# Second block's attention: query remainders on VectorE, weight remainders on GpSimd, third query set transposed later

## The chip, the cores and the metric

The kernel runs on one core of a Trainium2 chip. The metric is the device time of one execution, in microseconds (us). One core has TensorE (matrix products; "PE" in the rows, its weight loads "PEld"), VectorE ("DVE"), ScalarE ("ACT"), GpSimd ("POOL"), and SyncE ("SP"), which here starts DMA transfers. Each engine executes its own instructions in the order in which they stand in the program, and waits for the others by semaphores.

## The reference

The input is 512 tokens by 1024 features, all in f32. It goes through a first block (two layers of gated recurrent and convolutional mixing with a feed-forward part) and a second block. The change is in the attention of the second block:

```python
h = rmsnorm(x, attn_norm_w)
a_q, a_k, a_v, i_q, i_k, i_w, b_q, b_k, b_v, g_a, g_b = split(h @ w_in)
# a: 8 query heads of 64, i: 8 index heads of 64, b: 8 query heads of 64;
# keys and values have 4 heads; i_k is one head with a layer norm
a_q, a_k, i_q, i_k, b_q, b_k = rope(...)
o_a = dsa_branch(a_q, a_k, a_v, i_q, i_k, i_w, 128)  # each query attends to 128 keys, by index scores
o_b = swa_branch(b_q, b_k, b_v, sinks)               # sliding window with a sink per head
mix = sigmoid(g_a) * (o_a @ w_branch_a) + sigmoid(g_b) * (o_b @ w_branch_b)
x = x + mix @ w_out
```

A feed-forward part and a last norm follow.

## The kernel before

**Products in three parts.** Every f32 product is made of three matmuls of a reduced f32 type: high by high, high by low and low by high parts (lines 202, 203, 204). So each operand is split in two: a copy in the reduced type, and the remainder that the copy lost. Weights come in chunks of 128 x 1024 by DMA, four chunks ahead of their use. `prep` (line 173) splits a chunk: ScalarE copies it (line 178), and the remainder is made either by VectorE in one operation (`self.V`) or by GpSimd in pieces of 256 columns (line 182). Which of the two is written in the string `pool` of the stage's entry in `TUNE`: it lists the indices of the chunks that go to GpSimd, one string for each weight matrix. The entry of the second block's attention is the fifth, line 29. Its nine strings stand for the index queries (4 chunks), the keys (3), the values (2), the queries of branch b (4), those of branch a (4), the gates of branch b (four matrices of 2 chunks), the gates of branch a, and the two output matrices. Before, the first six are empty.

**Queries.** `q_proj` makes one set of queries: 4 token tiles of 128 x 512, accumulated in 4 banks of PSUM over 4 chunks of weights (24 matmuls a chunk). `q_hold` then evacuates each tile: `rotate` (line 1127) multiplies it by cosines and, in two halves, by sines (VectorE, tiles named t), adds the two (line 1136, on GpSimd where the flag `pool` is set), ScalarE copies the sum as the high part (line 1147), and line 1148 subtracts for the remainder, on GpSimd. `q_turn` (line 1152) transposes the held tiles (line 1160, 8 transposes into a bank of tag "py", of which there are two, in the order of use shared with the gates' matmuls), and evacuates each bank by ScalarE (line 1166) or by VectorE's CAST. There are three such sets: index queries, branch b ("s" tiles), branch a ("E" tiles).

**Order of the stage.** `block2` emits: index queries, keys, values, index scores, then the queries of branch b and of branch a, then a loop over four head pairs of branch b. Each pass takes two pending turns from the list `turns`, emits a gate (24 matmuls, p<-hT,w), the scores of the next pair (lines 1244 and 1245, two matmuls each, whose row sums VectorE makes with small operations on two columns, c, behind them), a second gate, and the values of the present pair: transposes of the probabilities (line 1373), VectorE's split of the transposed tile (E<-p,E), and the matmuls of lines 1325 to 1327. Eight gates make 192 matmuls.

**Selection in the background.** `select` (line 1267) finds the 128 largest index scores of each query: 16 rounds of MAX (line 1275) and MATCH_REPLACE (line 1276) on three score rows of 256, 384 and 512 columns, ended by line 1278. It is spawned behind the index scores, and `pump` (line 133) puts its steps between other work: a step is emitted when VectorE's booked time and the step's cost stay within TensorE's booked time plus a slack of 8 us. Every operation called through `self.V` (class `Paced`, line 55) books VectorE time; one on GpSimd books none. A scheduler then orders each engine's queue.

Of the kernel before, what the change touches and what calls it, by code (L numbers as in the profile page):

```python
# [13 lines left out]
OP = mybir.AluOpType  # L14
# [11 lines left out]
        dict(slack=0.0, tap=400, prep=20, fetch=-50, ada=100, aq=0, ak=1, af=1, bp=1000, pt=1, adma=-300, gap=3.0, pool=('01', '01'), mv=(), early=1, pin=0, go=0, ho=1),  # L26
        dict(slack=12.0, tap=400, prep=50, fetch=-200, ada=800, aq=0, ak=0, af=0, bp=200, pt=0, adma=100, gap=3.0, pool=('01', '01', '01', '01', '0'), mv=(1, 0, 0), early=1, pin=1, go=0, ho=1),
        dict(slack=10.0, tap=1500, prep=-30, fetch=0, ada=0, aq=0, ak=1, af=1, bp=0, pt=0, adma=100, gap=3.0, pool=('01', '1'), mv=(), early=0, pin=0, go=0, ho=1),
        dict(slack=8.0, tap=200, prep=50, fetch=-200, ada=300, aq=1, ak=0, af=0, bp=200, pt=0, adma=100, gap=6.0, pool=('', '', '', '', '', '', '012', '01', ''), mv=(), early=0, pin=0, go=0, ho=1),
        dict(slack=8.0, tap=200, prep=50, fetch=-200, ada=300, aq=1, ak=0, af=0, bp=200, pt=0, adma=100, gap=6.0, pool=('', ''), mv=(), early=0, pin=0, go=0, ho=1)]  # L30

COLS = {}
# [18 lines left out]
def f32(ap):  # L51
    return ap.bitcast(F32)
# [20 lines left out]
class Kern:  # L73
# [1068 lines left out]

    def q_hold(self, i, p, hold, tag):

        a = self.rotate(p.rearrange("p (h d) -> p h d", h=8), i, 8, True)
        q = self.tile(tag, (128, 8, 128), F32R)
        self.nc.scalar.activation(q[:, :, 0:64], a, AF.Copy)
        self.nc.gpsimd.tensor_tensor(q[:, :, 64:128], a, f32(q[:, :, 0:64]), op=OP.subtract)
        hold[i] = q

    def q_turn(self, i, hold, qt, hps):
# [244 lines left out]
    def block2(self):  # L1396
        nc, V = self.nc, self.V
        qi = self.q_proj("s")
        kt = self.k_proj()
        vs = self.v_proj()  # L1400
        self.work_turns()
        self.index_scores(qi, kt[0])
        self.selected = False
        self.spawn(self.select())
        qb = self.q_proj("s")
        qa = self.q_proj("E")
        gb = [self.tile("ad", (128, 2, T)) for _ in range(3)] + [self.tile("E", (128, 2, T))]
        gb = [gb[j // 2][:, j % 2] for j in range(8)]
        ob = []
        P = self.scores_b(0, qb, kt)  # L1410
        for hp in range(4):
            for _ in range(2):
                if self.turns:
                    self.turns.pop(0)()
            self.gate(gb[2 * hp], "py")
            Q = self.scores_b(hp + 1, qb, kt) if hp < 3 else None
            self.gate(gb[2 * hp + 1], "py")
            ob.append(self.values_b(hp, P, vs))
            P = Q
        self.drain(lambda: self.selected)  # L1420
        oa, wb, ga = [], [], []
        heads = [1, 0, 3, 2, 5, 4, 7, 6]
        P = self.scores_a(heads[0], qa, kt)
        o = None
        for n, h in enumerate(heads):
            if n % 2 == 0:
                g = self.tile("E", (128, 2, T))
                ga += [g[:, 0], g[:, 1]]
                o = self.bank(tag="py")
            p = self.branch(n, wb, ob)  # L1430
            V.scalar_tensor_tensor(gb[n], gb[n], 1.0, p, op0=OP.add, op1=OP.mult)
            Q = self.scores_a(heads[n + 1], qa, kt) if n < 7 else None
            self.gate(ga[n], "pc")
            self.values_a(h, P, o, vs)
            if n % 2:
                oa.append(self.out_T(o))
            P = Q
        for n, o in (("oa", oa), ("ob", ob)):
            for k in range(4):
                if self.dump is not None and n + str(k) in self.dump:  # L1440
                    t = self.t2()
                    V.tensor_tensor(t, f32(o[k][:, 0]), f32(o[k][:, 1]), op=OP.add)
                    self.dbg(n + str(k), t)
        if self.stop == "att":
            return
        mix, wa = [], []
        for j in range(8):
            p = self.branch(j, wa, oa)
            t = self.t2()
            V.scalar_tensor_tensor(t, ga[j], 1.0, p, op0=OP.add, op1=OP.mult)  # L1450
            nc.gpsimd.tensor_tensor(t, t, gb[j], op=OP.add)
            s = self.slot((128, 2, T), F32R)
            self.split(s[:, 0], s[:, 1], t, 0.5)
            mix.append(s)
        self.y = [self.tile("E" if i < 4 else "s", (128, D)) for i in range(4)]
        for i in range(4):
            nc.sync.dma_start(self.y[i], self.xsrc[i])
        self.n += 1
        dst = self.dram.tile([T, D], F32, name=f"xd{self.n}")
        self.xsrc = [dst[i * 128:(i + 1) * 128, :] for i in range(4)]  # L1460
        self.tok_group(lambda k, i: (mix[k][:, 0, i * 128:(i + 1) * 128], mix[k][:, 1, i * 128:(i + 1) * 128]),
                       False, True, self.add_norm(self.cols2[:, 8:16]))
        if self.stop == "b2":
            return
        self.tune = TUNE[5]
        self.ffn(self.final_norm, onto_x=True)
# [225 lines left out]
```

## Time and profile before

| | |
|---|---|
| median of 3 runs | 2317.67 us (2316.12 to 2319.96) |
| profiled execution | 2312.6 us, span 2310.9 us |
| mean granted TensorE clock | 0.988 of full speed |
| TensorE busy | 2217.4 us, 96% of the span |
| VectorE busy | 1470.7 us, 64% |
| ScalarE busy | 972.4 us, 42% |
| GpSimd busy | 718.9 us, 31% |

The shares are over the whole span. The attention of the second block lies between about 1545 and 1800 us; the changed instructions there are a small part of the span, so the stretch itself has to be read: windows for the shares by stretch, and the engines' timelines for what an engine waited for.

### The profile page before, as it was taken

The numbers are of one execution on the slowest core, as the hardware profiler recorded it, in microseconds if no ns is written. First come the engines' busy times: TensorE is split into PE (matmuls) and PEld (weight loads), VectorE is DVE, ScalarE is ACT, GpSimd is POOL, SyncE is SP. The second block draws the span as 40 slices with busy tenths as digits, with TensorE's granted clock in tenths as the row PEclk, the third lists the DMA queues.
The fourth block names the chain that finished last, engine by engine and source line by source line (L and its number), as shares of the span: only waits on it lengthen the run. The fifth ranks groups of instructions, "written<-read, shape, count | busy, mean of one in ns | idle before, by whom it ended". The sixth has DMA issues, their size and how long they took to land.

```text
span 2310.9 us, 29330 instructions
## 1 busy us (share of the span) xinstructions
PE 2217.4 (96%) x10744; PEld 1813.1 (78%) x10744; DVE 1470.7 (64%) x2939; ACT 972.4 (42%) x1697; POOL 718.9 (31%) x934
## 2 busy tenths in 40 slices
PE   5998999899999999999999999999989999999998
PEld 3677887788888787788778888878778888888886
DVE  6699999637676769999663333357996445443434
ACT  3435554533223454555543322344456534332232
POOL 4645561515325454655351210212112340000000
PEclk8999999999999999999999999999999999999999
DMA  7424226346666432222323323232111234222222
GB/s 285 160 92 137 64 87 205 128 143 216 210 203 210 140 119 86 70 65 73 121 101 128 113 91 100 93 100 90 62 55 56 64 108 152 105 99 93 92 100 82
DMA packets 77759, 271.39 MB, mean 117 GB/s; under 512 B 9008, under 2 KB 9776, under 8 KB 77616
## 3 DMA queue, kind: packets, MB, share of 16 engines
q1 hardware_dynamic: 69840, 241.21, 31.3%
q0 software_dynamic: 7776, 28.32, 3.7%
q8 instruction: 84, 1.38, 0.2%
q14 instruction: 59, 0.48, 0.1%
HBM read 256.91 MB, written 12.58 MB: 117 GB/s over the span
## 4 chain that ended last, share of the span: by engine, by line
PE 77%; DVE 10%; ACT 4%; POOL 3%; issue 3%; DMA 2%; SPq 0%; ACTq 0%; POOLq 0%; DVEq 0%
PE p L202 24%; PE p L204 24%; PE p L203 24%; DVE p L872 2%; POOL w L182 2%; DVE c L69 1%; ACT w L178 1%; DVE E L69 1%; DVE w L69 1%; DMA ad<-in_ada_dram 1%; PE p L1244 1%; DVE cc L69 1%; DMA wr<-in_win_dram 1%; DVE s L69 1%; DVE e L1276 1%
## 5 line engine op out<-in xcount | busy, mean ns | idle before, releaser
L182 POOL TENSOR_TENSOR w<-wr,w 128x256 fp32r<-128x256 f32 x648 | 502.6, 808 | 699.2 <-ACT w L178 619.1
L178 ACT ACTIVATE w<-wr 128x1024 fp32r<-128x1024 f32 (+1 forms) x353 | 369.7, 1049 | 610.5 <-PE p L204 525.0
L202 PE MATMUL p<-hT,w 128*128 128x512 f32 (+1 forms) x1568 | 586.6, 376 | 16.2 <-ACT hT L214 9.8
L203 PE MATMUL p<-hT,w 128*128 128x512 f32 (+1 forms) x1568 | 584.6, 373 | 9.2 <-POOL hT L218 5.4
L204 PE MATMUL p<-hT,w 128*128 128x512 f32 (+1 forms) x1568 | 585.0, 374 | 0.8 <-POOL w L182 0.7
L202 PE MATMUL p<-w,s 128*128 128x512 f32 (+1 forms) x1152 | 449.2, 390 | 3.5 <-ACT s L214 3.5
L203 PE MATMUL p<-w,s 128*128 128x512 f32 (+1 forms) x1152 | 448.0, 389 | 0.6 <-DVE w L69 0.6
L204 PE MATMUL p<-w,s 128*128 128x512 f32 (+1 forms) x1152 | 446.8, 389 | 0.1
L69 DVE TENSOR_TENSOR w<-wr,w 128x1024 fp32r<-128x1024 f32 (+1 forms) x187 | 234.4, 1254 | 294.2 <-ACT w L178 293.8
L202 PEld LDWEIGHTS p<-hT,w 128*128 128x128 f32 x1568 | 297.2, 190 | 72.5 <-ACT hT L214 11.6
L203 PEld LDWEIGHTS p<-hT,w 128*128 128x128 f32 x1568 | 298.3, 190 | 64.4 <-POOL hT L218 6.5
L872 DVE SCALAR_TENSOR_TENSOR p<-ga,ad,p 128x495 f32<-128x495 f32 (+24 forms) x480 | 339.0, 729 | 7.3 <-ACT p L867 6.3
L204 PEld LDWEIGHTS p<-hT,w 128*128 128x128 f32 x1568 | 298.5, 190 | 56.0 <-POOL w L182 3.7
L202 PEld LDWEIGHTS p<-w,s 128*128 128x128 f32 x1152 | 216.6, 188 | 52.6 <-ACT s L214 4.5
L204 PEld LDWEIGHTS p<-w,s 128*128 128x128 f32 x1152 | 216.3, 188 | 49.6 <-DVE s L69 1.1
L203 PEld LDWEIGHTS p<-w,s 128*128 128x128 f32 x1152 | 216.4, 188 | 48.7 <-DVE w L69 1.1
L69 DVE TENSOR_TENSOR E<-p,E 128x512 f32<-128x512 f32 (+4 forms) x152 | 94.9, 638 | 147.9 <-PE p L204 119.7
L69 DVE SCALAR_TENSOR_TENSOR t<-p,t 128x512 f32<-128x512 f32 x96 | 65.9, 687 | 128.8 <-ACT t L1066 128.7
L319 DVE SCALAR_TENSOR_TENSOR ad<-ad,ad 128x1024 f32<-128x1024 f32 x80 | 110.3, 1384 | 42.6 <-DMA ad<-in_ada_dram 42.6
L1066 ACT ACTIVATE t<-p 128x512 f32<-128x512 f32 x96 | 56.6, 589 | 157.6 <-PE p L204 157.6
L69 DVE TENSOR_TENSOR s<-t,s 128x512 fp32r<-128x512 f32 (+1 forms) x100 | 99.2, 992 | 11.1 <-ACT s L1068 5.7
L612 POOL TENSOR_TENSOR E<-E,s 128x512 f32<-128x512 f32 x32 | 46.4, 1460 | 155.4 <-ACT j L610 155.4
(279 smaller groups left out, 2622.3 us busy)
## 6 DMA issues: line engine op xcount, KB each, us to landing
wr<-in_ff_dram SPq DMA_DIRECT2D x128, 512.0 KB, 3.6
wr<-in_win_dram SPq DMA_DIRECT2D x64, 512.0 KB, 3.6
ad<-in_ada_dram POOLq DMA_DIRECT2D x54, 512.0 KB, 4.8
wr<-in_wout_dram SPq DMA_DIRECT2D x40, 512.0 KB, 3.6
wr<-in_up_dram SPq DMA_DIRECT2D x32, 512.0 KB, 3.7
wr<-in_down_dram SPq DMA_DIRECT2D x32, 512.0 KB, 3.3
ad<-in_ada_dram SPq DMA_DIRECT2D x26, 512.0 KB, 4.4
xd<-E SPq DMA_DIRECT2D x20, 512.0 KB, 2.7
```

The costliest lines, as they stand in the source:

```text
L69: return f(out, *a, **kw)
L178: self.nc.scalar.activation(u[:, 0, :w], raw[:, :w], AF.Copy)
L182: self.nc.gpsimd.tensor_tensor(u[:, 1, o:e], raw[:, o:e], f32(u[:, 0, o:e]), op=OP.subtract)
L202: mm(out, lh, rh, start=first, stop=False)
L203: mm(out, lh, rl, start=False, stop=False)
L204: self.mm = mm(out, ll, rh, start=False, stop=last)
L319: return self.nc.vector.scalar_tensor_tensor(w, w, 1.0, self.cact, op0=OP.mult, op1=OP.mult, accum_out=m)
L612: nc.gpsimd.tensor_tensor(y[:, h], y[:, h], row[:, h], op=OP.mult)
L872: V.scalar_tensor_tensor(y[:, d:], a[:, :T - d], w[:, o - d:o - d + 1], y[:, d:], op0=OP.mult, op1=OP.add)
L1066: nc.scalar.activation(r, p, AF.Relu)
L1244: mm(out, q[h // 2][:, h % 2, tk], k[:, 0, keys], start=True, stop=False)
L1276: V.match_replace(self.sel[i], m, self.sel[i], TAKEN)
```

## The change

Three things change. The strings `pool` of the stage send the remainders of 22 more weight chunks to GpSimd: two chunks of the index queries, all three of the keys, one of the values, all eight of the queries of b and a, and all eight of the gates of branch b (four weight matrices of two chunks each). The sum of the rotation and the remainder of the 12 query tiles go from GpSimd to VectorE. The loop over head pairs takes no turns in its first pass, so the transposes of the third query set begin one pass later. The DMA transfers keep their order.

```diff
-        dict(slack=8.0, ..., pool=('', '', '', '', '', '', '012', '01', ''), ...),
+        dict(slack=8.0, ..., pool=('01', '012', '0', '0123', '0123', '01', '012', '01', ''), ...),
...
     def q_hold(self, i, p, hold, tag):
 
-        a = self.rotate(p.rearrange("p (h d) -> p h d", h=8), i, 8, True)
+        a = self.rotate(p.rearrange("p (h d) -> p h d", h=8), i, 8)
         q = self.tile(tag, (128, 8, 128), F32R)
         self.nc.scalar.activation(q[:, :, 0:64], a, AF.Copy)
-        self.nc.gpsimd.tensor_tensor(q[:, :, 64:128], a, f32(q[:, :, 0:64]), op=OP.subtract)
+        self.V.tensor_tensor(q[:, :, 64:128], a, f32(q[:, :, 0:64]), op=OP.subtract)
         hold[i] = q
...
         for hp in range(4):
-            for _ in range(2):
+            for _ in range(2 if hp else 0):
                 if self.turns:
                     self.turns.pop(0)()
             self.gate(gb[2 * hp], "py")
```

**VectorE at the third query set.** Of before, from the set's first rotation (t<-p,gw; s is a bank of the second set's transposes, w a weight remainder, ga and c the scores' row sums):

```order
L69 TENSOR_TENSOR t_14865<-p_14630,gw_11084 128x512
L69 TENSOR_TENSOR t_14866<-p_14630,gw_11084 128x8x32 x2
L69 ISA ga_14879,c_14880<-p_14878,ad_11086 128x128
L69 ISA c_14880 128x1
L69 CAST s_14967<-p_14976 128x2x256
L69 ISA ga_14879,c_14880<-p_14878,ad_11086 128x128
L69 ISA c_14880 128x1
L69 TENSOR_TENSOR w_14994<-wr_14729,w_14994 128x1024
L69 TENSOR_SCALAR c_14881<-c_14880 128x2
L69 CAST s_14969<-p_14988 128x2x256
```

Of the new kernel, from the same set's rotations (t<-t,t is the sum, E the remainder):

```order
L69 TENSOR_TENSOR t_14928<-p_14693,gw_11084 128x8x32
L69 TENSOR_TENSOR t_14936<-p_14694,gw_11084 128x512
L69 TENSOR_TENSOR E_14924<-t_14918,E_14924 128x8x64
L69 TENSOR_TENSOR t_14927<-t_14927,t_14928 128x512
L69 TENSOR_TENSOR t_14937<-p_14694,gw_11084 128x8x32 x2
L69 TENSOR_TENSOR E_14933<-t_14927,E_14933 128x8x64
L69 TENSOR_TENSOR t_14936<-t_14936,t_14937 128x512
L69 TENSOR_TENSOR t_14945<-p_14695,gw_11084 128x512
L69 TENSOR_TENSOR t_14946<-p_14695,gw_11084 128x8x32
L69 TENSOR_TENSOR E_14942<-t_14936,E_14942 128x8x64
L69 TENSOR_TENSOR t_14946<-p_14695,gw_11084 128x8x32
L69 ISA ga_14959,c_14960<-p_14958,ad_11086 128x128
```

The sums and the remainders stand between the rotations on VectorE now, and the weight remainder w has gone.

**VectorE at the values of head pair 0.** Of before, the rows up to the first split (E<-p,E), with two banks of the third set's transposes (s) and a weight remainder:

```order
L1276 MATCH_REPLACE e_14307<-cc_15809,e_14307 128x384
L69 TENSOR_SCALAR c_14947<-c_14946 128x2
L69 CAST s_14967<-p_15208 128x2x256
L69 TENSOR_TENSOR c_14949<-ad_11086,c_14947 128x2
L69 TENSOR_TENSOR w_15226<-wr_14997,w_15226 128x1024
L69 TENSOR_TENSOR c_14949<-c_14949,c_14948 128x2
L69 CAST s_14969<-p_15220 128x2x256
L69 RECIPROCAL c_14950<-c_14949 128x2
L69 ISA ga_15026,c_15027<-p_15025,ad_11086 128x128
L69 ISA c_15027 128x1
L69 TENSOR_TENSOR E_15150<-p_15145,E_15150 128x512
```

Of the new kernel, the rows up to the first split:

```order
L1278 TENSOR_SCALAR e_14333<-e_14333 128x256
L1276 MATCH_REPLACE e_14333<-cc_15922,e_14333 128x512
L69 TENSOR_TENSOR c_15129<-c_15129,c_15128 128x2
L1278 TENSOR_SCALAR e_14333<-e_14333 128x384
L69 RECIPROCAL c_15130<-c_15129 128x2
L69 ISA tc_15147,c_15148<-p_15146,ad_11086 128x256
L69 ISA c_15148 128x1
L1278 TENSOR_SCALAR e_14333<-e_14333 128x512
L69 ISA tc_15147,c_15148<-p_15146,ad_11086 128x256
L69 ISA c_15148 128x1
L69 TENSOR_SCALAR c_15149<-c_15148 128x2
L69 TENSOR_TENSOR E_15208<-p_15203,E_15208 128x512
```

and from the last split to the first bank of the third set's transposes:

```order
L69 TENSOR_TENSOR E_15248<-p_15245,E_15248 128x2x128
L69 TENSOR_SCALAR c_15347<-c_15346 128x2
L69 TENSOR_TENSOR c_15349<-ad_11086,c_15347 128x2
L69 TENSOR_TENSOR c_15349<-c_15349,c_15348 128x2
L69 RECIPROCAL c_15350<-c_15349 128x2
L69 ISA z_15367,c_15368<-p_15366,ad_11086 128x256
L69 ISA c_15368 128x1
L69 TENSOR_TENSOR s_15257<-p_15202,s_15257 128x512
L69 CAST s_15261<-p_15270 128x2x256
```

The end of selection (L1278) now stands ahead of the first split (before, 35 of its 99 rows stand behind), and the second bank's CAST, which stood ahead of the first split, stands behind the last.

**TensorE ahead of the 49th gate matmul.** Of before (p<-identr,E are transposes of the third query set; the gate matmul is p<-hT,w, and the 48th is a few rows up):

```order
L1160 MATMUL p_15220<-identr,E_14862 128x128
L1160 MATMUL p_15220<-identr,E_14871 128x128
L1160 MATMUL p_15220<-identr,E_14862 128x128
L1160 MATMUL p_15220<-identr,E_14871 128x128
L1325 MATMUL p_15144<-E_15150,s_14291 128x256
L202 MATMUL p_15231<-hT_13496,w_14782 128x512
```

Of the new kernel, where values and scores of pair 1 fill the place between the 48th and the 49th:

```order
L1326 MATMUL p_15202<-E_15248,s_14329 64x128
L1327 MATMUL p_15202<-E_15248,s_14329 64x128
L1373 MATMUL p_15473<-identr,z_15125 128x128
L1373 MATMUL p_15473<-identr,tc_15147 128x128
L1373 MATMUL p_15473<-identr,z_15125 128x128
L1373 MATMUL p_15473<-identr,tc_15147 128x128
L1244 MATMUL p_15366<-E_14064,s_14730 128x256
L1245 MATMUL p_15366<-E_14064,s_14730 128x256
```
```order
L1160 MATMUL p_15282<-identr,E_14933 128x128
L1160 MATMUL p_15282<-identr,E_14924 128x128
L1160 MATMUL p_15282<-identr,E_14933 128x128
L202 MATMUL p_15296<-hT_13502,w_14853 128x512
```

Before, 23 rows lie between the 48th and the 49th gate matmul; now 93 do.

## Rows read from the trace of the kernel before

**Rows 1.** Windows: length; busy us (count) PE, PEld, DVE, ACT, POOL; clock, DMA, GB/s.
```profile
1650.00:1675.00 25.00, 24.33 (x115) 19.52 (x114) 21.75 (x50) 7.53 (x10) 11.14 (x8) 1.00 0.19 68
1675.00:1700.00 25.00, 19.52 (x96) 16.10 (x94) 19.92 (x53) 8.75 (x19) 10.19 (x8) 0.80 0.18 65
1690.00:1695.00 5.00, 4.89 (x21) 4.19 (x20) 4.51 (x9) 2.51 (x8) 3.07 (x3) 0.50 0.25 90
1700.00:1725.00 25.00, 23.35 (x137) 19.25 (x135) 24.71 (x93) 18.22 (x53) 0.00 (x0) 1.00 0.12 43
```

**Rows 2.** TensorE's timeline: start us, length, line, operation, form [idle before, releaser].
```profile
1591.85 0.37 PE L1160 MATMUL p<-identr,s 128*128 128x128 f32 x2 [2.08 <-ACT s L1166]
...
1681.03 0.40 PE L204 MATMUL p<-w,hT 128*128 128x512 f32 x1
...
1685.65 0.34 PE L1160 MATMUL p<-identr,E 128*128 128x128 f32 x2 [1.71 <-ACT s L1166]
...
1689.16 1.00 PE L1160 MATMUL p<-identr,E 128*128 128x128 f32 x6 [2.87 <-POOL E L1148]
...
1692.78 0.79 PE L202 MATMUL p<-hT,w 128*128 128x512 f32 x1
...
1706.75 0.39 PE L204 MATMUL p<-hT,w 128*128 128x512 f32 x1
...
1711.57 0.50 PE L202 MATMUL p<-hT,w 128*128 128x512 f32 x1
...
1765.75 0.40 PE L204 MATMUL p<-hT,w 128*128 128x512 f32 x1
```

**Rows 3.** GpSimd's timeline: query sums and remainders, then weight pieces.
```profile
1682.14 1.27 POOL L1136 TENSOR_TENSOR t<-t,t 128x512 f32<-128x512 f32 x1 [15.30 <-DVE t L69]
...
1692.32 1.49 POOL L1148 TENSOR_TENSOR E<-t,E 128x512 fp32r<-128x512 f32 x1 [0.74 <-ACT E L1147]
...
1742.19 3.42 POOL L182 TENSOR_TENSOR w<-wr,w 128x256 fp32r<-128x256 f32 x4 [48.38 <-DVE c L69]
...
1752.79 2.81 POOL L182 TENSOR_TENSOR w<-wr,w 128x256 fp32r<-128x256 f32 x4 [7.17 <-ACT w L178]
```

**Rows 4.** VectorE's timeline, from the second query set to the end of selection.
```profile
1652.69 3.54 DVE L69 TENSOR_TENSOR t<-p,gw 128x512 f32<-128x512 f32 x8
...
1680.72 3.53 DVE L69 TENSOR_TENSOR t<-p,gw 128x512 f32<-128x512 f32 x8
...
1690.20 0.69 DVE L69 CAST s<-p 128x512 fp32r<-128x512 f32 x1 [2.49 <-PE p L1160]
...
1692.59 1.24 DVE L69 TENSOR_SCALAR c<-c 128x2 f32<-128x2 f32 x1
...
1719.89 0.41 DVE L69 TENSOR_TENSOR E<-p,E 128x256 fp32r<-128x256 f32 x1
...
1743.54 0.71 DVE L69 TENSOR_TENSOR c<-c,c 128x2 f32<-128x2 f32 x1
```

**Rows 5.** VectorE's groups, 1600 to 1770 us: count | busy us, mean ns | idle before.
```profile
L69 DVE TENSOR_TENSOR w<-wr,w 128x1024 fp32r<-128x1024 f32 x15 | 19.0, 1264 | 2.2 <-ACT w L178 2.2
L1275 DVE MAX8 cc<-e 128x8 f32<-128x384 f32 x16 | 8.8, 549 | 0.0
L1276 DVE MATCH_REPLACE8 e<-cc,e 128x384 f32<-128x384 f32 x16 | 8.7, 541 | 0.0
L1276 DVE MATCH_VALUE_LOAD e<-cc,e 128x8 f32 x48 | 3.8, 80 | 0.0
L69 DVE CAST s<-p 128x512 fp32r<-128x512 f32 x9 | 6.1, 680 | 2.5 <-PE p L1160 2.5
L69 DVE TENSOR_TENSOR t<-p,gw 128x256 f32<-128x256 f32 x16 | 6.0, 414 | 1.1 <-POOL t L1136 1.1
L69 DVE CUSTOM_DVE_ANT_0 tc<-p,ad 128x256 f32<-128x256 f32 x12 | 5.7, 471 | 1.7 <-PE p L1245 1.7
L69 DVE TENSOR_TENSOR c<-ad,c 128x2 f32<-128x2 f32 x16 | 2.4, 149 | 0.2
```

More of the change, by code (lines that the diff above doesn't have):

```diff
@@ L28 @@
         dict(slack=10.0, tap=1500, prep=-30, fetch=0, ada=0, aq=0, ak=1, af=1, bp=0, pt=0, adma=100, gap=3.0, pool=('01', '1'), mv=(), early=0, pin=0, go=0, ho=1),
-        dict(slack=8.0, tap=200, prep=50, fetch=-200, ada=300, aq=1, ak=0, af=0, bp=200, pt=0, adma=100, gap=6.0, pool=('', '', '', '', '', '', '012', '01', ''), mv=(), early=0, pin=0, go=0, ho=1),
+        dict(slack=8.0, tap=200, prep=50, fetch=-200, ada=300, aq=1, ak=0, af=0, bp=200, pt=0, adma=100, gap=6.0, pool=('01', '012', '0', '0123', '0123', '01', '012', '01', ''), mv=(), early=0, pin=0, go=0, ho=1),
         dict(slack=8.0, tap=200, prep=50, fetch=-200, ada=300, aq=1, ak=0, af=0, bp=200, pt=0, adma=100, gap=6.0, pool=('', ''), mv=(), early=0, pin=0, go=0, ho=1)]
```

## The prediction

> **What bounds the kernel now.** I read the page for the shares first: TensorE is busy in 96% of the span, so only places where it stands still or runs slowly can give time, and a change on VectorE and GpSimd costs time only where TensorE comes to wait for them. The windows show where that is. From 1650 to 1675 us TensorE is full and VectorE nearly so; from 1675 to 1700 TensorE has 19.52 us of 25 at a mean clock of 0.80, and from 1700 to 1725 VectorE is the fullest engine with 24.71 of 25 [rows 1]. TensorE's timeline names the waits: 1.71 us for a ScalarE copy and 2.87 us for GpSimd's remainder L1148, with small ones between; from the third query set's last matmul, at 1681.03, to the first gate matmul at 1692.78 almost nothing but short transposes and scores runs, and the gate matmuls start 0.43 us apart instead of 0.23, at the clock of 0.50 that the window 1690 to 1695 shows, 1.2 GHz [rows 1, 2]. GpSimd's timeline shows the cause: the four sums (L1136) and remainders (L1148) of the third set take it from 1682.14 to 1693.8 without a pause worth naming, and each is waited for by ScalarE's copy, by the transposes and by VectorE, whose scratch it holds [rows 3].
>
> Behind that, VectorE sets the pace. The first split of a probability tile (values of head pair 0) starts right after its queue of scores, selection rounds and weight remainders; its last split is at 1719.89, and the row at 1743.54 is the first behind the end of selection [rows 4]. The 48th gate matmul has started by 1706.75 and the 49th starts at 1711.57: only 48 gate matmuls (two gates) stand ahead of the values of pair 0, and the next gate waits for banks that VectorE empties [rows 2].
>
> **Prices.** Rows of VectorE overlap by about 0.08 us: the row of 3.53 us at 1680.72 is three 512-wide and five 256-wide operations (the order shows them), and three of 0.60 and five of 0.33 with one overhang make 3.53 [rows 4, 5]. So from start to start a 512-wide operation costs 0.60, a 256-wide 0.33, a MAX 0.47 (mean of the three lengths: the 384-wide row is their middle, 549 ns less 0.08), a MATCH_REPLACE with its load 0.53, a row sum over 256 columns 0.39 (over 128 0.26, by size), an operation on two columns 0.07, and a 1024-wide weight remainder 1.18 [rows 5]. GpSimd needs 2.81 to 3.42 us for the four pieces of one chunk [rows 3].
>
> **The change, part by part.**
> *Weights.* 22 chunks leave VectorE, at 1.18 us 26 us (the 984- and 656-wide ones a little less), and cost GpSimd about 22 x 3.1 = 68 us over the 200 us that the second block's attention takes. A chunk feeds 24 matmuls (5.6 us at 0.233), so GpSimd keeps up; where it starts late (the key projection's three chunks, whose chain of small operations TensorE waits for), a chunk is ready about 2 us later than on VectorE. I take +1, between 0 and +4.
> *Query sets.* 24 operations of 512 columns come to VectorE, 24 x 0.60 = 14.4 us, and leave GpSimd (1.27 to 1.49 each). The first set's stall of 2.08 us at 1591.85 [rows 2] becomes about 0.5: -1.5. The third set no longer holds up the gates: the 11 us between 1681 and 1692.78 and the slow start behind it (nine gate matmuls at +0.20, 1.8 us) go as they stand.
> *What is late next.* The emitter places selection rounds by the VectorE time it has booked. Remainders on GpSimd book none, so the rounds come earlier. In the order of before 35 of selection's 99 rows stand behind the first split of pair 0; in the new order all 99 stand ahead of it, as do the row sums of pair 1. I counted VectorE's queue from the first rotation of the third set to the last split of pair 0:
> before, 13 MAX 6.1, 13 MATCH_REPLACE 6.9, 3 weight remainders 3.5, 5 bank copies 3.0, rotations 5.0, 12 row sums 4.2, splits 2.1, 23 small 1.6: 32.4 us. The trace has 39.6 (1680.72 to 1720.30), of which about 5.1 are idle, 2.49 in one piece [rows 4], 1.1 one disturbed small operation (below), and 1.0 scatter.
> after, 20 MAX 9.4, 20 MATCH_REPLACE 10.6, rotations 5.0, 8 sums and remainders 4.8, 20 row sums 7.0, splits 2.1, 36 small 2.5, the end of selection 0.9, one bank copy 0.6: 42.9 us.
> Seven more operations (1.8 us) lead to the bank copy behind which the 49th gate matmul gets its banks, 44.7. Add the scatter 1.0; idle 1.0 (0 to 4; the GpSimd waits are gone); and what GpSimd's pieces take from VectorE. The row for that: at 1692.59 an operation on two columns took 1.24 us instead of 0.15 while GpSimd ran a remainder, and at 1743.54 one took 0.71 beside weight pieces [rows 3 to 5]. In 45 us GpSimd runs four or five chunks, 30% of the time, against some 35 operations that can meet a piece, each losing about half a piece of 0.75: 3.6, and 0 if they never meet; I take 3. That makes 49.7 us, between 45 and 55.
> The Trainium skill ("SBUF — State Buffer", Who interferes with whom) says that a VectorE instruction with two SBUF inputs and a GpSimd instruction that reads SBUF exclude each other for the whole of whichever starts first. The trace agrees (1.24 and 0.71 us against 0.15). Without the rule the sum would be 3 us less.
> *When that queue starts.* The third set's rotation began at 1680.72, 28.0 us after the second's at 1652.69 [rows 4], as TensorE's matmuls allow. VectorE's queue between the two grows from 21.2 to 25.5 us (8 sums and remainders come, 4 weight remainders go, 3 more selection rounds); with scatter and contention 28.5, so it still starts about then. With the shift of the earlier part (+1 and -1.5, and up to 1 for the 0.5 by which VectorE is now late): 1681.2, between 1678.5 and 1685.
> *TensorE meanwhile.* In the new order gates 0 and 1 follow the third set at once and end near 1696. Between the 48th and the 49th gate matmul stand 8 us of transposes, scores and values, all of which follow VectorE. So the 49th starts at 1681.2 + 49.7 + 0.5 = 1731.4 instead of 1711.57: +19.8. TensorE idles some 25 us in between, against about 12 now (with the half clock).
> *What comes back.* From the 49th gate matmul to the last (192nd, 1765.75) before takes 54.2 us [rows 2], of which TensorE's own work is 33.6 for 144 gate matmuls and 13.7 for 149 short ones. In the new order 51 of the short ones have moved ahead of the 49th, so 8.6 remain, and selection is over, so VectorE no longer presses: 42.2 of work and about 3 of waits, 45.3: -8.9 (between -11.9 and -5). After the long idle stretch the clock may be at 1.2 GHz for some matmuls, as in rows 2: +0.8 (0 to 1.8).
> Sum: +19.8 - 8.9 + 0.8 = **+11.7 us**. The profiled execution took 2312.6 us (span 2310.9) and would take 2324.3; the median of the runs is 2317.67, so I predict **2329 us**. The ends of the terms, not all at once, give +4 to +20: 2322 to 2338.
>
> **Rivals.**
> *Faster: the GpSimd wait was the bound.* If the queue on VectorE is shorter than I counted, because the scheduler's order lets splits of pair 0 meet their data early or selection is further along than its rows suggest, then what remains is the gain: the 4.6 us of waits at 1685.65 and 1689.16, small ones of 2, the slow clock 1.8 and 1.5 at 1591.85, together about -9, less 1 to 3 for weights that come late: -7, 2310.5 us. For it speaks that the longest idle stretch of TensorE in this stage names GpSimd; against it that VectorE has 24.71 of 25 us in the next stage and gets 10 us more to do before the splits. It decides if the 49th gate matmul starts before about 1716.
> *No change.* VectorE needs 45 us instead of 49.7 (no contention, no idle time) and 11.9 us come back instead of 8.9: 15.1 - 11.9 = +3, 2321. The row 1700 to 1725 speaks for a VectorE that has no slack, so only the end terms lead here.
> *Slower elsewhere.* GpSimd is late in the key projection and for the gates' weights, as each chunk takes 3 us on it and waits behind the previous one: 22 chunks x 0.5 to 1 us: +11 to +22 with the gates at their old time, 2329 to 2340. Against it: 5.6 us of matmuls a chunk, and four chunks of weights fetched ahead.
> *Both late*: the count and GpSimd's delays add up, +20 to +28, 2338 to 2346.
>
> **How the numbers follow.** 0.2%, 4.6 us, is about what a measurement of this kernel can tell from no change: below 2313.0 is faster, above 2322.3 slower. My sum (+4 to +20) gets 0.58, of which 0.05 falls below +4.6; the faster rival 0.15, of which 0.02 ends within 0.2%; no change 0.12; late weights alone 0.08; both late 0.07. Faster 0.13, same 0.19, slower 0.68. The range for 8 in 10 goes from 2312 (leaving out most of the faster rival) to 2340.
>
> **What would show it.** Right: TensorE's timeline of the new kernel has gate matmuls from about 1683, an idle stretch of 20 us or more in pieces between the 48th and 49th, broken by values L1325 to L1327 that wait for VectorE; the first split of pair 0 stands after L1278 and later than 1722; the 49th gate matmul starts between 1725 and 1738, and the last 42 to 49 us later; VectorE is busy over 22 of 25 us from 1680 to 1725, and operations on two columns take 0.3 to 0.7 us beside GpSimd's pieces. Wrong: the 49th before 1716 (the count of the queue failed), waits for L182 on TensorE of more than 5 us in all (weights late), or a third set that begins its rotation later than 1686 (the earlier part moved).

## The result, and the profile after

The changed kernel takes 2332.42 us (median of 4 runs, 2330.79 to 2334.17) against 2318.49 us before: 13.9 us by the medians, whose quotient is 1.0060. The ratio on record is 1.0072, 95% interval 1.0059 to 1.0084; the profiled executions differ by 18.2 us (2330.79 against 2312.6). Slower was forecast, at 2329 us, with 11.7 us more for the change.

On the page TensorE's busy time has hardly moved, and its share of the span has fallen by a point; one slice of the row of clocks now reads 7:

```profile
PE 2220.9 (95%) x10744; PEld 1814.9 (78%) x10744; DVE 1477.2 (63%) x2941; ACT 972.5 (42%) x1697; POOL 749.2 (32%) x997
PEclk9999999999999999999999999999979999999999
```

The windows of the new kernel answer to [rows 1] (columns as there):

```profile
1650.00:1675.00 25.00, 25.00 (x119) 20.34 (x118) 24.83 (x64) 8.14 (x11) 13.80 (x18) 1.00 0.31 100
1675.00:1700.00 25.00, 23.72 (x119) 19.23 (x118) 24.82 (x67) 8.61 (x17) 11.58 (x15) 1.00 0.23 73
1700.00:1725.00 25.00, 10.27 (x39) 6.54 (x38) 23.72 (x98) 12.56 (x42) 2.79 (x4) 0.59 0.10 33
1725.00:1750.00 25.00, 21.39 (x107) 17.54 (x108) 14.11 (x55) 17.05 (x49) 2.83 (x4) 0.86 0.00 1
```

From 1675 to 1700 TensorE is nearly full (23.72 of 25 us) at full clock, where before it had 19.52 us at 0.80. The next window has paid for it: 10.27 us of work at a mean clock of 0.59, with VectorE busy for 23.72 of 25. TensorE's timeline, which answers to [rows 2], shows the third set's last matmul, the first gate matmul, the 48th, transposes of the third set, two of the waits, the last of them, further transposes, the 49th gate matmul and the 192nd:

```profile
1684.78 0.39 PE L204 MATMUL p<-w,hT 128*128 128x512 f32 x1
...
1686.94 0.50 PE L202 MATMUL p<-hT,w 128*128 128x512 f32 x1 [0.59 <-ACT s L1166]
...
1700.52 0.40 PE L204 MATMUL p<-hT,w 128*128 128x512 f32 x1
...
1702.28 0.53 PE L1160 MATMUL p<-identr,E 128*128 128x128 f32 x4 [1.08 <-ACT ad L1384]
...
1708.23 0.58 PE L1244 MATMUL p<-E,s 128*128 128x256 f32 x1 [2.82 <-DVE c L69]
...
1725.95 0.58 PE L1244 MATMUL p<-E,s 128*128 128x256 f32 x1 [2.23 <-DVE c L69]
...
1737.94 0.39 PE L1244 MATMUL p<-E,s 128*128 128x256 f32 x1 [0.95 <-DVE c L69]
...
1739.14 0.54 PE L1160 MATMUL p<-identr,E 128*128 128x128 f32 x4 [0.40 <-DVE s L69]
1739.51 0.47 PE L202 MATMUL p<-hT,w 128*128 128x512 f32 x1
...
1784.65 0.40 PE L204 MATMUL p<-hT,w 128*128 128x512 f32 x1
```

The first gate matmul follows the third set's last by 2.16 us (before 11.75), and the 48th is over at 1701. Then TensorE stands, for 2 to 3 us at a time, for VectorE's row sums, whose last operation writes tile c, until the 49th at 1739.51, 39 us behind the 48th. On VectorE, answering to [rows 4], the second and third sets' first rotations, two disturbed operations, a wait, the last operation of a row sum (the TensorE wait at 1725.95 ends with it), the end of selection, three of the splits of pair 0, a wait for ScalarE, and the bank copy that the 49th gate matmul follows:

```profile
1656.96 1.94 DVE L69 TENSOR_TENSOR t<-p,gw 128x512 f32<-128x512 f32 x4
...
1683.49 1.93 DVE L69 TENSOR_TENSOR t<-p,gw 128x512 f32<-128x512 f32 x4
...
1688.41 1.23 DVE L69 TENSOR_TENSOR t<-t,t 128x512 f32<-128x512 f32 x1
...
1696.08 0.70 DVE L69 TENSOR_SCALAR c<-c 128x2 f32<-128x2 f32 x1
...
1717.92 0.48 DVE L69 CUSTOM_DVE_ANT_0 tc<-p,ad 128x256 f32<-128x256 f32 x1 [0.42 <-PE p L1245]
...
1725.82 0.08 DVE L69 DVE_READ_ACCUMULATOR2_ANT c<- 128x1 f32 x1
1725.82 0.42 DVE L1278 TENSOR_SCALAR e<-e 128x512 f32<-128x512 f32 x1
...
1727.41 0.69 DVE L69 TENSOR_TENSOR E<-p,E 128x512 fp32r<-128x512 f32 x1
...
1730.32 0.69 DVE L69 TENSOR_TENSOR E<-p,E 128x512 fp32r<-128x512 f32 x1 [0.97 <-ACT E L214]
...
1735.38 0.42 DVE L69 TENSOR_TENSOR E<-p,E 128x256 fp32r<-128x256 f32 x1
...
1737.13 0.16 DVE L69 TENSOR_TENSOR c<-c,c 128x2 f32<-128x2 f32 x1 [1.06 <-ACT c L1355]
...
1738.40 0.68 DVE L69 CAST s<-p 128x512 fp32r<-128x512 f32 x1
```

The end of selection stands ahead of the first split, and the copy of the turns' second bank behind the last, as in the order. That bank was filled at 1702.28 (four transposes fill a bank, not eight); its copy is over at 1739.08, and only then, at 1739.14, do the transposes run behind which the 49th gate matmul stands in TensorE's queue. GpSimd's pieces of two chunks, answering to [rows 3], cost 3.75 us where VectorE runs sums and remainders beside them and 2.79 where it runs selection:

```profile
1686.48 3.75 POOL L182 TENSOR_TENSOR w<-wr,w 128x256 fp32r<-128x256 f32 x4 [3.47 <-ACT w L178]
...
1703.26 2.79 POOL L182 TENSOR_TENSOR w<-wr,w 128x256 fp32r<-128x256 f32 x4 [5.10 <-ACT w L178]
```

To find where the time went I take four stretches of each profiled execution, between starts of matmuls that its timeline shows: from the last matmul of the previous block's feed-forward part to the third query set's last; from there to the 49th gate matmul; from there to the 192nd; and on to the span's end. In us:

| kernel | to third set's end | to 49th gate | to 192nd | to the end | sum |
|---|---|---|---|---|---|
| before | 131.96 | 30.54 | 54.18 | 545.15 | 761.83 |
| new | 134.39 | 54.73 | 45.14 | 544.45 | 778.71 |
| turns alone | 132.56 | 56.35 | 47.53 | 545.72 | 782.16 |
| turns undone | 133.84 | 31.10 | 52.96 | 545.78 | 763.68 |
| weights alone | 140.24 | 32.84 | 54.25 | 546.07 | 773.40 |
| queries alone | 128.36 | 26.01 | 54.29 | 547.44 | 756.10 |
| new, booked | 133.63 | 53.45 | 45.13 | 544.00 | 776.21 |
| queries, late weights | 128.74 | 29.88 | 53.33 | 545.96 | 757.91 |
| queries, turns between | 130.04 | 17.80 | 60.06 | 551.80 | 759.70 |
| new, turns between | 133.36 | 20.37 | 59.68 | 546.92 | 760.33 |
| queries, index weights | 129.65 | 25.56 | 54.29 | 548.63 | 758.13 |
| queries, key weights | 131.42 | 26.32 | 54.42 | 547.09 | 759.25 |
| queries, gate weights | 129.24 | 27.96 | 55.85 | 545.72 | 758.77 |
| queries, late weights, turns between | 130.50 | 19.15 | 60.14 | 547.60 | 757.39 |

A sum differs from the span by what lies ahead of the first mark, which the change doesn't touch and which moved by 4 us from one execution to the next; so stretches are compared, and ratios of the timed runs decide. Each ratio below is to the kernel before as it was timed beside that experiment: a median of 2316.54 us for the first four, 2315.00 for the next four and 2314.85 for the last four. The new kernel loses 24.2 us ahead of the 49th gate matmul and 2.4 in the earlier stretch, and gets 9.0 back.

### The profile page after: what moved, and what is told of

The parts are those of the page before. It is cut to its first block, busy times and chain, and to the rows that moved or that the text cites. A ratio compares the mean times of both kernels' runs of the same rounds, so it can differ in the third digit from the quotient of the medians.

```text
span 2329.1 us, 29382 instructions
## 1 busy us (share of the span) xinstructions
PE 2220.9 (95%) x10744; PEld 1814.9 (78%) x10744; DVE 1477.2 (63%) x2941; ACT 972.5 (42%) x1697; POOL 749.2 (32%) x997
## 4 chain that ended last, share of the span: by engine, by line
PE 78%; DVE 11%; ACT 4%; DMA 3%; POOL 2%; issue 2%; ACTq 0%; SPq 0%; DVEq 0%; POOLq 0%
PE p L202 24%; PE p L204 24%; PE p L203 24%; DVE p L872 2%; POOL w L182 2%; DVE c L69 2%; ACT w L178 1%; DMA ad<-in_ada_dram 1%; DVE E L69 1%; DVE ad L319 1%; DVE s L69 1%; DVE cc L69 1%; PE p L1244 1%; DMA wr<-in_win_dram 1%; DVE e L69 0%
## 5 line engine op out<-in xcount | busy, mean ns | idle before, releaser
L182 POOL TENSOR_TENSOR w<-wr,w 128x256 fp32r<-128x256 f32 x735 | 566.5, 803 | 798.9 <-ACT w L178 763.2
L69 DVE TENSOR_TENSOR w<-wr,w 128x1024 fp32r<-128x1024 f32 x165 | 205.9, 1248 | 288.4 <-ACT w L178 288.1
L204 PEld LDWEIGHTS p<-w,s 128*128 128x128 f32 x1152 | 216.5, 188 | 49.7 <-DVE s L69 1.3
L319 DVE SCALAR_TENSOR_TENSOR ad<-ad,ad 128x1024 f32<-128x1024 f32 x80 | 122.1, 1532 | 45.6 <-DMA ad<-in_ada_dram 45.6
L69 DVE TENSOR_TENSOR s<-t,s 128x512 fp32r<-128x512 f32 (+1 forms) x108 | 105.7, 979 | 13.2 <-ACT s L1147 4.9
```

Of the source, the lines that this page charges most:

```text
L69: return f(out, *a, **kw)
L182: self.nc.gpsimd.tensor_tensor(u[:, 1, o:e], raw[:, o:e], f32(u[:, 0, o:e]), op=OP.subtract)
L204: self.mm = mm(out, ll, rh, start=False, stop=last)
L319: return self.nc.vector.scalar_tensor_tensor(w, w, 1.0, self.cact, op0=OP.mult, op1=OP.mult, accum_out=m)
```

## The experiments

The forecast's reason was that weight remainders on GpSimd book no VectorE time, so that selection is placed early and holds up the values (theory A). The new order allowed another: the turns, moved behind the values of pair 0 in the program, take the gates' two banks with them (theory B). No run gave the turns banks of their own; the experiments move the turns, and what the banks have to do with it is read from the order and the timelines.

**Turns alone.**

```diff
 # on the kernel before
-            for _ in range(2):
+            for _ in range(2 if hp else 0):
```

> The kernel before with only the loop's change: no turns in the first pass; weights on VectorE and query sums and remainders on GpSimd as before. Theory A (the one on record: weight remainders on GpSimd book no VectorE time, so selection is placed ahead of the values of pair 0 and holds them up): the weights are booked again, so the 49th gate matmul stays within 5 us of before's 1711.6 and the time is 2310 to 2322 us. Theory B (the turns' place in the loop does it: emitted behind the values of pair 0, they and the next gates, which take the same two banks, queue behind them): 49th gate matmul later than 1727, time 2325 to 2340 us.

Measured: 2336.59 us, ratio 1.0090 (1.0076 to 1.0103). The 48th and 49th gate matmuls and one of the waits between them, from TensorE's timeline:

```profile
1706.11 0.39 PE L204 MATMUL p<-hT,w 128*128 128x512 f32 x1
...
1713.54 0.58 PE L1244 MATMUL p<-E,s 128*128 128x256 f32 x1 [3.00 <-DVE c L69]
...
1741.65 0.69 PE L202 MATMUL p<-hT,w 128*128 128x512 f32 x1 [0.35 <-ACT s L1166]
```

and on VectorE the first split, the end of selection, and the turns' copy:

```profile
1728.93 0.69 DVE L69 TENSOR_TENSOR E<-p,E 128x512 fp32r<-128x512 f32 x1
...
1738.94 0.69 DVE L1278 TENSOR_SCALAR e<-e 128x384 f32<-128x384 f32 x2
...
1739.54 0.69 DVE L69 CAST s<-p 128x512 fp32r<-128x512 f32 x1
```

With every weight remainder on VectorE, and booked, the 49th is as late as in the new kernel. Theory A falls: this one part of the change costs 20 us by itself, more than the whole. Nor need selection be over for it: here the first split stands 10 us ahead of selection's end. What the two kernels share is that TensorE has no gate to run while it waits, and that the turns' copy stands behind the splits of pair 0.

**Turns undone.**

```diff
 # on the new kernel
-            for _ in range(2 if hp else 0):
+            for _ in range(2):
```

> The new kernel with the loop as before (two turns in every pass); weights on GpSimd, query sums and remainders on VectorE. Theory A: still slow, 2325 to 2335 us, as the queue of VectorE ahead of the first split keeps the selection rounds that the weights no longer space out. Theory B: the 49th gate matmul starts within 6 us of 1711.6 (plus the 3.75 us by which the third set now ends later), the GpSimd stall behind the third set is gone, 2308 to 2320 us.

Measured: 2319.71 us, ratio 1.0016 (1.0007 to 1.0024). First, 48th and 49th gate matmuls:

```profile
1697.03 0.76 PE L202 MATMUL p<-hT,w 128*128 128x512 f32 x1
...
1710.57 0.39 PE L204 MATMUL p<-hT,w 128*128 128x512 f32 x1
...
1716.16 0.45 PE L202 MATMUL p<-hT,w 128*128 128x512 f32 x1
```

The 49th is 5.6 us behind the 48th instead of 39. Of the new kernel's loss 12.7 us (2332.42 less 2319.71; 1.0072 less 1.0016 by the ratios) is the turns' place. A loss of 3.2 us remains, so the other two parts together don't help either.

**Weights alone.**

```diff
 # on the kernel before
-pool=('', '', '', '', '', '', '012', '01', '')
+pool=('01', '012', '0', '0123', '0123', '01', '012', '01', '')
```

> The kernel before with only the weight strings changed: 22 more chunks on GpSimd, query sums and remainders still there too, turns as before. Theory A: slower, 2325 to 2340 us. Theory B: the weights cost what the earlier stretch of the new kernel lost (the third set ended 3.75 us later) and what GpSimd's pieces take from the query sums on the same engine: 2318 to 2328 us. A third view (GpSimd's pieces block VectorE and that is most of the loss): two-column operations of 0.5 us and more all through 1650 to 1725, over 2328 us.

Measured: 2326.88 us, 1.0045 (1.0032 to 1.0058): at the upper end of theory B's range, and just inside theory A's, so the time doesn't tell them apart. The 49th gate matmul, from TensorE's timeline, and the first split, from VectorE's, do:

```profile
1725.08 0.50 PE L202 MATMUL p<-hT,w 128*128 128x512 f32 x1
```

```profile
1726.04 0.68 DVE L69 TENSOR_TENSOR E<-p,E 128x512 fp32r<-128x512 f32 x1
```

All but 6 of selection's 99 rows stand ahead of the first split here, nearly as in the new kernel, and yet the 49th runs 4.6 us behind the 48th, ahead of the split. Early selection by itself doesn't hold up the gate. By the table the time is lost mostly in the earlier stretch (140.24 us against 131.96), where GpSimd does both the query sums and the weight pieces. Of the ways tried to split the two jobs with the turns in their old place this is the dearest.

**Queries alone.**

```diff
 # on the kernel before
-        a = self.rotate(p.rearrange("p (h d) -> p h d", h=8), i, 8, True)
+        a = self.rotate(p.rearrange("p (h d) -> p h d", h=8), i, 8)
...
-        self.nc.gpsimd.tensor_tensor(q[:, :, 64:128], a, ...)
+        self.V.tensor_tensor(q[:, :, 64:128], a, ...)
```

> The kernel before with only the query sums and remainders moved to VectorE; weights on VectorE, turns as before. Theories A and B agree that the stall of 4.6 us behind the third set and the 2 us at 1591.85 go; VectorE gets 14 us more to do and loses nothing. If VectorE's queue sets the 49th gate matmul (both theories) it starts 3 to 8 us later than 1711.6 and the time is 2312 to 2324 us; if the stall was the bound, 2306 to 2312 us.

Measured: 2310.96 us, 0.9975 (0.9966 to 0.9984): faster. The third set's last matmul, the remainder's wait, the first and the 49th gate matmul:

```profile
1679.16 0.39 PE L204 MATMUL p<-w,hT 128*128 128x512 f32 x1
...
1683.10 0.62 PE L1160 MATMUL p<-identr,E 128*128 128x128 f32 x5 [1.58 <-DVE E L69]
...
1688.05 0.76 PE L202 MATMUL p<-hT,w 128*128 128x512 f32 x1
...
1705.17 0.47 PE L202 MATMUL p<-hT,w 128*128 128x512 f32 x1
```

The wait of 2.87 us for GpSimd is one of 1.58 for VectorE, and the 49th comes 26.0 us behind the set instead of 30.5, not later: the stall was the bound, and 14.4 us more of VectorE work cost TensorE less than the stall had. The earlier stretch gains 3.6 us.

**The weights booked.**

```diff
 # on the new kernel, in prep's loop over pieces
                     e = min(o + PIECE, w)
+                    self.dt = max(self.dt, self.pt) + (e - o) / 960 if self.tune is TUNE[4] else self.dt
```

> The new kernel, in which the pieces on GpSimd book VectorE time by their width, as the remainder on VectorE did; nothing else. Theory A (selection is early because the weights aren't booked): the 49th gate matmul comes back to 1712 to 1722 us, time 2312 to 2322. Theory B (the turns' place in the loop): nothing that matters moves, 2328 to 2336 us, 49th gate matmul later than 1735.

Measured: 2329.43 us, 1.0057 (1.0042 to 1.0072), 48th and 49th gate matmuls:

```profile
1698.97 0.40 PE L204 MATMUL p<-hT,w 128*128 128x512 f32 x1
...
1737.17 0.47 PE L202 MATMUL p<-hT,w 128*128 128x512 f32 x1
```

Booking the pieces leaves the 38 us between them, and all but 3 of selection's rows still stand ahead of the first split. In the new order it is not the booking that makes the 49th late.

**Late weights.**

```diff
 # on the new kernel with the turns undone
-pool=('01', '012', '0', '0123', '0123', '01', '012', '01', '')
+pool=('', '', '', '0123', '0123', '01', '012', '01', '')
```

> The new kernel with two things undone: turns in every pass as before, and on GpSimd only the weights of the queries of b and a and of the gates of b (those of the index queries, keys and values are back on VectorE). Beside it stand the run with all weights on GpSimd (2319.71 us) and the one with none of them (2310.96), which differ by 8.75 us. If the loss by the weights is lateness in the early stretch (the norm's products behind the first chunks on GpSimd, the key projection): 2310 to 2314 us, and from the last matmul of the previous block's feed-forward part to the third set's last the run without weights' 128.4 us, within 1. If it is GpSimd's pieces blocking VectorE from 1640 on: 2316 to 2321 us, with 31 us instead of 26 from the third set's last matmul to the 49th gate matmul.

Measured: 2313.10 us, 0.9986 (0.9978 to 0.9995). The early stretch is back at 128.74 us, as expected from lateness there, and the stretch behind the third set takes 29.88 instead of 26.01, near the 31 expected from GpSimd's pieces; the latter is given back over the next two stretches but for 1.4 us. Selection also runs earlier here (22 of its rows stand behind the first split, 46 with the queries alone), which could delay the splits as well; the two causes weren't told apart. The chunks of the index queries, keys and values cost 7 us of the weights' 9 (1.0016 against 0.9986).

**Turns between, queries alone.**

```diff
 # on the kernel with the queries alone
             self.gate(gb[2 * hp + 1], "py")
+            for _ in range(2):
+                if self.turns:
+                    self.turns.pop(0)()
             ob.append(self.values_b(hp, P, vs))
```

(and the same three lines taken from the pass's start)

> The run with only the queries' sums and remainders on VectorE (2310.96 us, first gate matmul 8.9 us behind the third set's last matmul), with the turns of every pass moved behind its second gate and ahead of its values. Theory B: the two gates of the first pass now run directly behind the third set, and the turns still stand ahead of the values, so the next gates aren't held up; 4 to 7 us less than without the move, 2304 to 2307 us. If VectorE's queue ahead of the values sets the 49th gate matmul whatever TensorE does before: no change, 2309 to 2313. Theory A has no reason for a change of more than 2 us.

Measured: 2312.28 us, 0.9985 (0.9975 to 0.9994): no gain, and rather a loss, on 0.9975; theory B's 2304 to 2307 us was missed. The 49th gate matmul comes 8.2 us earlier behind the third set, as theory B has it, but the next stretch takes 5.8 us more and the last 4.4 more. In the next stretch most of it is work that has moved there: 174 short matmuls stand between the 49th and the 192nd instead of 150, and TensorE is busy for 57.31 us of the stretch instead of 52.43. Behind it the window from 1750 to 1775 (columns as above) and the longest wait, from TensorE's timeline, show TensorE out of gates to put under the work of the others:

```profile
1750.00:1775.00 25.00, 21.49 (x125) 18.04 (x124) 16.16 (x58) 16.72 (x48) 6.10 (x8) 0.93 0.18 60
```

```profile
1765.58 0.39 PE L1325 MATMUL p<-E,s 128*128 128x256 f32 x1 [2.10 <-ACT E L214]
```

The 192nd gate matmul starts at 1761.10, and behind it TensorE waits 0.49 and 2.10 us for scores and splits that VectorE and ScalarE haven't delivered; the kernel with the queries alone has 24.22 us of TensorE in this window. So what the earlier gates won went to short matmuls that now follow the 49th, and to waits behind the last gate; where the rest of the 4.4 us went stays open.

**Turns between, all parts.**

```diff
 # on the new kernel
-            for _ in range(2 if hp else 0):
-                if self.turns:
-                    self.turns.pop(0)()
             self.gate(gb[2 * hp], "py")
...
             self.gate(gb[2 * hp + 1], "py")
+            for _ in range(2):
+                if self.turns:
+                    self.turns.pop(0)()
```

> The new kernel with its turns behind the second gate of each pass and ahead of the values, in the first pass too; all weights on GpSimd. Against the new kernel (2332.42 us) theory B expects the whole loss of the turns back and what the earlier gates bring: 2313 to 2319 us. Theory A, in which the unbooked weights hold up the values: 2326 to 2333 us.

Measured: 2314.07 us, 0.9992 (0.9983 to 1.0002). First, 48th and 49th gate matmul, and on VectorE the turns' second copy and the first split:

```profile
1685.49 0.50 PE L202 MATMUL p<-hT,w 128*128 128x512 f32 x1 [0.59 <-ACT s L1166]
...
1699.09 0.39 PE L204 MATMUL p<-hT,w 128*128 128x512 f32 x1
...
1703.70 0.65 PE L202 MATMUL p<-hT,w 128*128 128x512 f32 x1
```

```profile
1703.67 0.68 DVE L69 CAST s<-p 128x512 fp32r<-128x512 f32 x1
...
1711.12 0.69 DVE L69 TENSOR_TENSOR E<-p,E 128x512 fp32r<-128x512 f32 x1
```

The first turns still come after the first two gates, as the new kernel wants them, and all weights are on GpSimd; only the turns' place in the loop has changed, and 18 us are back (1.0072 less 0.9992 by the ratios). The copy stands ahead of the first split again. That the turns' place is the cause is shown from both sides: in the three kernels whose turns follow the values the 49th gate matmul is 35 to 39 us behind the 48th, in the eleven others 3.3 to 5.6.

**Which early weights.**

```diff
 # on the kernel with the queries alone; first kernel, second kernel
-pool=('', '', '', '', '', '', '012', '01', '')
+pool=('01', '', '', '', '', '', '012', '01', '')
+pool=('', '012', '', '', '', '', '012', '01', '')
```

> The run with only the queries moved (2310.96 us, ratio to before 0.9975), with two chunks more on GpSimd: the first two of the index queries, whose pieces stand ahead of the last two products of the norm (L612) on GpSimd. All early weights together (index queries, keys, values) lost 6 to 7 us (ratio 1.0016 against 0.9986 without them). If the loss is the norm's products behind these two chunks: ratio 0.999 to 1.000. If it is the keys' chunks: 0.997 to 0.998, as without.

> The run with only the queries moved (ratio 0.9975), with the three chunks of the keys on GpSimd, where they run beside the first query set's sums and remainders on VectorE. If the loss of the early weights is GpSimd's and VectorE's blocking of each other there (the sums took 1.1 to 1.3 us instead of 0.69, the chunks 3.6 instead of 2.8, in the run with all weights): 0.9990 to 1.0005, key matmuls 3 us later behind the previous block's last matmul. If it is the norm's products: 0.997 to 0.998.

Measured: 0.9977 (0.9969 to 0.9986) and 0.9978 (0.9968 to 0.9988). Neither is told apart from 0.9975, though the profiled executions show 1.3 and 3.1 us more in the early stretch; the losses that one reading or the other expected did not come. Neither group alone accounts for the 7 us; which mixture does (the value chunk wasn't tried alone, nor two groups at once) stays open.

**Gate weights.**

```diff
 # on the kernel with the queries alone
-pool=('', '', '', '', '', '', '012', '01', '')
+pool=('', '', '', '', '', '01', '012', '01', '')
```

> The run with only the queries moved (ratio 0.9975), with the eight chunks of the gates of branch b on GpSimd. It takes 9.4 us off VectorE where VectorE is full (1690 to 1770). If VectorE's load there costs time: 0.995 to 0.997. If GpSimd's pieces take as much from VectorE as they relieve it of: 0.9970 to 0.9985. Theory A (unbooked weights hold up the values): 0.999 or more.

Measured: 0.9982 (0.9973 to 0.9991): GpSimd takes as much as it relieves. Theory A's 0.999 lies just inside the interval, so this run alone doesn't tell against it.

**Late weights, turns between.**

```diff
 # on the new kernel with the turns between
-pool=('01', '012', '0', '0123', '0123', '01', '012', '01', '')
+pool=('', '', '', '0123', '0123', '01', '012', '01', '')
```

> Turns behind the second gate of each pass, queries on VectorE, and on GpSimd the weights of the queries of b and a and of the gates of b. The run with all weights and this place of the turns gained 5.5 us on the same with turns first; without the early weights another 6 should go: 0.9965 to 0.9975, the same as or a little better than the run with only the queries moved. If what the earlier gates bring is given back later, as in the run with this place of the turns and no weights moved: 0.998 to 0.999.

Measured: 2308.02 us, 0.9975 (0.9965 to 0.9985). It and the kernel with the queries alone are the same 0.25% below the kernel before; the plainer of them is the version to keep.

## Why the prediction was right, and where it was wrong

**The sum.** The forecast had +19.8 us to the 49th gate matmul, -8.9 back and +0.8: +11.7. By the table the profiled execution has 2.4 and 24.2 us to the 49th, -9.0 back and -0.7 behind the 192nd, +16.9 in all, inside the range of +4 to +20. The number was counted from the new order, which was at hand, so it needed no reason for that order and doesn't confirm the one that was given.

**The GpSimd stall goes: right, but not by the part it was put down to.** Gates start 2.16 us behind the third set, at full clock. Moving the sums and remainders doesn't do that by itself: with the queries alone the first gate matmul comes 8.88 us behind the set, with the turns undone 11.98 (1685.06 to 1697.03), both still 0.43 us apart at first, and the waits for GpSimd have become waits for VectorE. With the turns alone, the sums still on GpSimd, it comes 4.51 us behind. Most of the earlier start is the turns' place: the transposes no longer stand ahead of the gates.

**VectorE's queue sets the 49th gate matmul: in the range, and wrong in cause.** From the third set's first rotation to the bank copy I counted 44.7 us and added 1.0 scatter, 1.0 idle and 3 for GpSimd, 49.7. The trace has 54.9 (1683.49 to 1738.40), and the 49th started at 1739.51, 1.5 us behind the 1725 to 1738 given as the sign; TensorE's idle time ahead of it came to 18.3 us in pieces, not 20 or more. The missing 5.2 is idle time of VectorE: 6.7 us where I had put 1.0. Of it 2.6 are waits for TensorE's scores (0.42 us or more at five of them; one row stands above), which come late while a score's matmul takes 0.58 us (0.39 at 1737.94); 2.0 are waits for ScalarE's copies of two split tiles, and 1.6 for its exponentials (line 1355); without the idle time the stretch is 0.5 shorter than counted. I had let VectorE run without a gap because the GpSimd waits were gone; once TensorE has nothing but what VectorE feeds it, each waits for the other. The term for GpSimd was too dear. In the new kernel, from 1640 to 1745:

```profile
L69 DVE TENSOR_TENSOR t<-t,t 128x512 f32<-128x512 f32 x8 | 6.5, 810 | 0.0
L69 DVE TENSOR_SCALAR c<-c 128x2 f32<-128x2 f32 x11 | 2.7, 242 | 0.1
```

Against 684 and 155 ns with the queries alone, that is 8 x 0.13 + 11 x 0.09 = 2.0 us in both groups over 105 us. Three readings of mine were off without weight in the sum. The row of 1.24 us that I set beside the rule for two SBUF inputs has one such input and a constant (line 1351); the row of 0.71 has two. Thirty-five operations that meet a piece 30% of the time and lose half of 0.75 us come to 3.9 us, not 3.6. And VectorE's queue between the second and third sets' rotations before, given as 21.2 us, comes to 24.0 by my prices and the trace's rows; the 25.5 for the new kernel, which the sum used, holds.

The step that failed is the one that takes "remainders on GpSimd book none, so the rounds come earlier" for the reason why the 49th gate matmul is late. Selection does come earlier where weight remainders leave VectorE: of its 99 rows 46 stand behind the first split with the queries alone, 21 with all weights moved too (turns undone). But the 49th is 5.6 us behind the 48th there, and with the weights alone, 6 rows behind, 4.6. Booking the remainders changed nothing for it, and the same lateness came without a single weight moved. The place of the turns in the loop did it, which I had listed among the edits and given no price of its own. Why the scheduler then lays so much of selection ahead of the splits was not settled.

**The return: right.** 45.3 us forecast from the 49th to the 192nd, 45.14 measured.

**The earlier stretch: both terms too small.** I gave -1.5 for the first set and +1 for late weights (and up to 1 for a VectorE that is late). The queries alone gained 3.6 us there, and all weights on top of them cost 5.5 (133.84 against 128.36): +1.9 instead of -0.5, near the 2.4 of the new kernel.

**The rivals.** "The GpSimd wait was the bound" was not what happened to the whole change, but it is what happened to its query part: 5.6 us less (ratio 0.9975), where the rival had 7. I had given it 0.15 because VectorE was full in the next stretch. In that stretch the gates covered VectorE's lateness; a full engine costs nothing while the one that waits for it has something else to do.

## What to carry to other kernels

Price each part of a change alone before the sum: here the queries (-5.6 us), the weights on top of them (+8.7) and the turns on top of both (+12.7) stood in one edit, and the largest was the one line that had no price. When independent matmuls fill the waits of a chain, look in the instruction order for what stands between them: here moving work that shares their banks behind the chain took the filler away. A reason found for an order is a theory until the order has been changed by it; here that could be tried without touching a single instruction's cost.

## What the runs showed of the hardware

VectorE operations and GpSimd pieces lengthened each other. From 1570 to 1600 us VectorE's sums of two tiles, beside GpSimd's weight pieces (turns undone), and without them (queries alone):

```profile
L69 DVE TENSOR_TENSOR t<-t,t 128x512 f32<-128x512 f32 x4 | 4.7, 1169 | 0.0
```

```profile
L69 DVE TENSOR_TENSOR t<-t,t 128x512 f32<-128x512 f32 x4 | 2.7, 685 | 0.0
```

1169 ns instead of 685, while the pieces of one chunk took 3.6 to 3.75 us instead of 2.8. This agrees with the Trainium skill ("SBUF — State Buffer", Who interferes with whom), which has a VectorE instruction with two SBUF inputs and a reading GpSimd instruction exclude each other. MAX and MATCH_REPLACE kept their durations (547 and 540 ns for 384 columns in the new kernel from 1640 to 1725, against 549 and 541 in [rows 5]).

The operations on two columns with one SBUF input were lengthened too: 242 ns in the mean beside 155, and 0.70 us for the one at 1696.08, while GpSimd ran a chunk's pieces.

TensorE's granted clock was 0.59 in the mean, between its two levels of 1.2 and 2.4 GHz, in the window in which it worked 10.27 us of 25 in short pieces, and 1.00 from the 49th gate matmul to the 192nd, in which it worked without a pause worth naming (columns as for the windows above):

```profile
1739.51:1784.65 45.14, 44.85 (x243) 37.72 (x243) 16.69 (x57) 24.70 (x64) 14.11 (x20) 1.00 0.15 47
```
